# A GeGLU MLP on one core: four reorderings (pending gelu, w_down sums, first pair, last product)

## The chip, the cores and the metric

The kernel runs on one core of a Trainium2 chip. The metric is the device time of one execution in microseconds (us); three runs of the kernel before gave 2256.16, 2256.80 and 2257.91, median 2256.8.

## The reference

```python
x: (8, 1024, 1024)   w_gate, w_up: (1024, 4096)   w_down: (4096, 1024)   # float32
gate = x @ w_gate
up = x @ w_up
gate = 0.5 * gate * (1 + np.tanh(np.sqrt(2 / np.pi) * (gate + 0.044715 * gate ** 3)))
h = gate * up
return (h @ w_down).astype(np.float32)
```

## The kernel before, in words

**Passes.** The 8192 tokens are worked off in 8 passes of 1024 (`NPASS`, `TOK`). Each pass computes h for its tokens ("gate and up") and then the output ("down"). Operands are float16, sums are float32 in PSUM. The matrix products are done with fewer block products than the plain way, by sums and differences of blocks: passes 0 to 2 split every operand into 2x2 blocks and use 7 products in place of 8 (`gate_up_one`, `down`); passes 3 to 7 use operands split further, with 26 products for a group of four pairs' blocks (`gate_up_fast`, `quad`, `down_fast`). The operands of the later passes (sums of weight blocks) are made on the way in passes 0 to 2 and stored in DRAM: `wdop` from `wd_sums`/`wd_store` in pass 0, `wop` from `make_entry` in passes 1 and 2, `wdq` from `wd_unit`.

**Engines.** TensorE multiplies. ScalarE (ACT) copies PSUM banks, applies gelu and makes some entries; VectorE (DVE) adds PSUM to temporaries and forms operand sums; GpSimd (POOL) multiplies gelu by up and issues the weight loads (L336) and w_down loads (L394); SP issues the other transfers. Each engine executes its instructions in the order in which the program issues them: the order is written out by hand (`tc.manual_schedule()`, L241), and semaphores that the framework adds between engines do the waiting.

**A pair (L602 to L675).** In passes 0 to 2, one of the 16 pairs i of a pass covers two blocks of 128 gate and up columns. `SEQ` (L551) lists its 14 products: a name P1 to P7 and w (0 gate, 1 up). A product is 4 matmuls of 128x128 weights by 512 tokens (L626). It adds into the PSUM bank of its chain: P1, P6, P7, P4 share chain a, P5 and P3 chain b, P2 goes to chain c. After product k, `AFTER1` (L555) lists what the other engines do:

- after P1: "copy 0" and "copy 1" (L642, ScalarE): the bank of chain a is copied to a new bank c. P6, products 4 and 5, adds onto the a bank, so it must wait for these copies.
- P2 adds onto the banks that the copies wrote. In `SEQ` it stands late; the second pair of pass 0 uses `SEQ0` (L570), in which P2 makes products 3 and 4.
- "snap" (L637, ScalarE): a bank to a temporary; "add" (L645, VectorE): a bank plus a temporary; "gelu" (L650) and "gelu11", "gelu21" (L658), both ScalarE; "h11", "h21" (L663, VectorE); "prod" (L652, GpSimd).
- the last two, "add s2 0" and "add s2 1", come after products 13 and 14, the last of the pair. What follows them, "gelu s2" and "prod s2", is put into `pending` (L675) and issued by `flush()` in the next pair, after its product 2 and both copies (L671).

Between these stand `extra` steps: `sum_w` (L351, VectorE) forms the four weight sums of the next pair, in even pairs after products 3, 5, 7, 9, in odd pairs after 11 to 14; in passes 1 and 2 `make_entry` (L278 on VectorE, L374 on ScalarE) makes an entry after every second product, and `wd_unit` adds sums of its own (L278, L506).

**w_down in pass 0 (L708 to L719).** For n = 0 to 3, `wd_load` (four loads, GpSimd), `wd_sums` (four VectorE sums, L410 to L416) and `wd_store` (seven stores, SP) stand at slot s0 + ds, where slot 14 i + k is product k of pair i. With s0 = 28 n + 72 the sums stand in the even pairs 6, 8, 10 and 12.

**The first pair (L1191 to L1273)** of pass 0 starts from float32 inputs in DRAM. Loads of x and of the first weight columns are issued by SP at the start (L1275 to L1283); VectorE casts x (L297), TensorE transposes it (L303), VectorE and ScalarE copy the transposed blocks to SBUF (L305, L307), ScalarE casts weights (L331), and `products(mh, kh, c)` multiplies (L1198). The token half mh = 1 is transposed in two portions, each between two groups of products. `outputs` (L1210, L1211) makes the first blocks of h.

**The end (`down_fast`, L1063 to L1187).** `DOWN` (L118) lists products ("mul", 16 x 2 matmuls of 256 columns, L1099, both token halves m of one entry j after the other) and what is done with their banks: "snap" (L1156, ScalarE) and "acc" (L1168, VectorE), which adds a bank to a temporary; an "acc" with a last number of 0 or more is final, and its store (L1111, SP) is issued after the next product (`todo`). After the last product ("mul" 23) stand three final accs: two of the bank of product 22, then one of its own bank.

Of the kernel before, what the change touches and what calls it, by code (L numbers as in the profile page):

```python
# [11 lines left out]
ADD = mybir.AluOpType.add  # L12
SUB = mybir.AluOpType.subtract
# [8 lines left out]
OSC = 16.0  # L22
# [151 lines left out]
def kernel(  # L174
# [422 lines left out]
    def flush():  # L597
        for f in pending:
            f()
        pending.clear()  # L600

    def pair(p, i, extra, seq, after):  # L602
        bank = {}
        t = {}

        def ps(b, w):
            return ps_all[:, bank[b, w]]

        def tl(n):
            t[n] = tmp_free.popleft()  # L610
            return tmp[:, t[n]]

        def product(name, w):
            b = CHAIN[name]
            first = name in ("P1", "P5")
            if first:
                bank[b, w] = ps_free.popleft()
            o = W_OPERAND[name]
            if isinstance(o, tuple):
                e = (i % 2) * 2 * P + o[1] * P  # L620
                lhs = raw(p, i // 2)[:, w, o[0] * KH : (o[0] + 1) * KH, e : e + P]
            else:
                lhs = ssum(i)[:, o, w]
            rhs = xq[X_OPERAND[name]]
            for k in range(KH):
                nc.tensor.matmul(  # L626
                    ps(b, w), lhs[:, k], rhs[:, k, :],
                    start=(first and k == 0), stop=(k == KH - 1),
                    skip_group_check=True,
                )  # L630

        def do(what):
            op, *a = what.split()
            n = a[0] if a else None
            w = int(a[1]) if len(a) > 1 else 0
            if op == "snap":
                nc.scalar.copy(tl((n, w)), ps("a", w))  # L637
            elif op == "copy":

                w = int(n)  # L640
                bank["c", w] = ps_free.popleft()
                nc.scalar.copy(ps("c", w), ps("a", w))  # L642
            elif op == "add":
                o = tmp[:, t[n, w]]
                nc.vector.tensor_tensor(o, ps("b", w), o, ADD)  # L645
                if n == "s2":
                    ps_free.append(bank["b", w])
            elif op == "gelu":
                o = tmp[:, t[n, 0]]
                nc.scalar.activation(o, o, GELU, scale=GSC)  # L650
            elif op == "prod":
                nc.gpsimd.tensor_tensor(  # L652
                    hq[TO[n]][:, i, :], tmp[:, t[n, 1]], tmp[:, t[n, 0]], MUL
                )
                tmp_free.extend((t[n, 0], t[n, 1]))
            elif op in ("gelu11", "gelu21"):
                b = "c" if op == "gelu11" else "a"
                nc.scalar.activation(tl(b), ps(b, 0), GELU, scale=GSC)  # L658
                ps_free.append(bank[b, 0])
            elif op in ("h11", "h21"):  # L660
                b = "c" if op == "h11" else "a"
                h = hq["a11" if op == "h11" else "a12"]
                nc.vector.tensor_tensor(h[:, i, :], ps(b, 1), tmp[:, t[b]], MUL)  # L663
                tmp_free.append(t[b])
                ps_free.append(bank[b, 1])

        for k, (name, w) in enumerate(seq, 1):
            product(name, w)
            for what in after.get(k, ()):
                do(what)  # L670
            if k == 2:  # L671
                flush()
            for f in extra.get(k, ()):
                f()
        pending.extend([lambda: do("gelu s2"), lambda: do("prod s2")])  # L675
# [4 lines left out]
    def gate_up_one(p):  # L680
        unit_steps = {}
        if p in UNITS_ONE:
            free = deque(xc[:, j * 512 : (j + 1) * 512] for j in range(32, 38))
            free.append(spare)
            for u, s0, ds in UNITS_ONE[p]:
                load, fs = wd_unit(u, xc[:, 12288:16384], free)
                unit_steps[s0] = load
                for k, f in enumerate(fs):
                    unit_steps[s0 + 36 + ds * k] = f
        for i in range(NP):  # L690
            q, e = divmod(i, 2)
            extra = {k: [] for k in range(1, 15)}

            def at(k, f, *a):
                extra[k].append(lambda: f(*a))

            if p == 0 and i == 0:
                first_pair()
                continue
            if p == 0:  # L700
                if e == 1:
                    at(13, load_raw, p, q + 2)
                if 11 <= i < 15:
                    at(7, half_load, 0, 2 * (i - 11))
                if i >= 14:
                    at(4, half_load, 1, 4 * (i - 14))
                    at(6, half_load, 1, 4 * (i - 14) + 2)
                for n in range(4):  # L708

                    s0 = 28 * n + 72  # L710
                    for ds, f, a in (
                        (0, wd_load, (n, 0)), (2, wd_load, (n, 1)),
                        (4, wd_load, (n, 2)), (6, wd_load, (n, 3)),
                        (22, wd_sums, (0,)), (23, wd_sums, (1,)),
                        (24, wd_sums, (2,)), (25, wd_sums, (3,)), (26, wd_store, (n,)),
                    ):
                        pr, k = divmod(s0 + ds - 1, 14)
                        if pr == i:
                            at(k + 1, f, *a)  # L719
            elif i == 0:  # L720
                at(1, load_raw, p, 1)
            elif e == 1:

                at(13, load_raw, p, q + 2)

            ks = (3, 5, 7, 9) if e == 0 else (11, 12, 13, 14)
            for n, k in enumerate(ks):
                at(k, sum_w, p, i + 1, n)

            if FAST - 2 <= p < FAST:  # L730
                for j, n in enumerate(entries_of(p - FAST + 2)):
                    if j // 6 == e:
                        at(2 * (j % 6) + 2, make_entry, p, q, n)
            if (p, i) in ((0, 2), (FAST - 1, 13)):
                at(8, cast_x, p + 1)
            for k in range(14):
                if 14 * i + k in unit_steps:
                    at(k + 1, unit_steps[14 * i + k])
            if i == NP - 2:
                order[0] = [0, 1, 4, 2, 3, 5] if p % 2 == 0 else [2, 3, 4, 0, 1, 5]  # L740
                if p:
                    at(2, load_d, p, 0)
                    at(3, load_d, p, 1)
            if i == NP - 1:
                at(1, load_d, p, 2 if p else 0)
            second = p == 0 and i == 1
            pair(p, i, extra, SEQ0 if second else SEQ, AFTER0 if second else AFTER1)


# [313 lines left out]
    def down_fast(p):  # L1063
# [27 lines left out]
                ]  # L1091
            )

        def product(e, js):
            _, entry, h, c, first = e
            lhs, rhs = place[h], q_chunk(entry)
            for j in js:
                for m in range(2):
                    nc.tensor.matmul(  # L1099
                        ps_all[:, bank[c], m * MQ : (m + 1) * MQ],  # L1100
                        lhs[:, j, m * P : (m + 1) * P],
# [25 lines left out]
                product(e, js)  # L1127
        if p + 1 < NPASS:
            transpose_x(p + 1)
        count = 0  # L1130
        for i, e in enumerate(DOWN):
            if e[0] == "mul":
                count += 1
                if count > 2:
# [56 lines left out]
    def first_pair():  # L1191
        bank = {(mh, j, w): 4 * mh + 2 * j + w for mh in range(2) for j in range(2) for w in range(2)}

        def products(mh, kh, c):
            for w in range(2):
                for j in range(2):
                    for k in range(KH):
                        nc.tensor.matmul(  # L1198
                            ps_all[:, bank[mh, j, w], c],
                            raw(0, 0)[:, w, kh * KH + k, j * P : (j + 1) * P],  # L1200
                            xq[f"b{kh + 1}{mh + 1}"][:, k, c],
                            start=(kh == 0 and k == 0 and c.start == 0),
                            stop=(kh == 1 and k == KH - 1),
                            skip_group_check=True,
                        )

        def outputs(mh, j):
            t = tmp_free.popleft()
# [26 lines left out]
            f()  # L1235
        for w in range(2):
            cast_first(w, 1, slice(0, 256), nc.vector.tensor_copy)
        for kh in range(2):
            products(0, kh, slice(0, MH))
        for g in range(2):  # L1240
            x0_cast(1, g)
        for g in range(2):
            x0_transpose(1, g, 6 + g)
        for g in range(2, G):
            x0_cast(1, g)
        outputs(0, 0)
# [2 lines left out]

        nc.gpsimd.tensor_copy(mark, staging0(1, 0)[:, 0, 256:257])  # L1250
        load_raw(0, 1)
        for kh in range(2):
            products(1, kh, slice(0, MQ))
        for g in range(2, G):
            x0_transpose(1, g, g - 2)
        outputs(0, 1)
        for w in range(2):
            cast_first(w, 1, slice(256, 512))
# [64 lines left out]
```

## Time and profile before

| what | value |
| --- | --- |
| median of 3 runs | 2256.8 us |
| the profiled execution: time | 2256.16 us |
| the profiled execution: span | 2254.4 us |
| granted TensorE clock, mean | 1.000 |
| TensorE (PE) busy | 2246.1 us, 16634 matmuls |
| VectorE (DVE) busy | 1561.7 us |
| ScalarE (ACT) busy | 956.1 us |
| GpSimd (POOL) busy | 679.3 us |
| pass 1, gate and up / pass 2 | 193.39 us each |
| first matmul / end of the last | 1.59 us / 2250.1 us |

A line of a timeline gives the start in us, the time the group of instructions took in us, the engine, the line of the kernel, the operation, what it writes and reads, shapes and count; in brackets stands how long the engine had been idle and what ended that. A row of the waits gives who waited for whom, the total in us, how many times, and the longest. A row of the chain that ended last gives start and length in us, then engine, tile and line. A name such as L848 is a line of the code above; SPq and POOLq are transfers that these engines issue.

### The profile page before, as it was taken

The numbers are of one execution on the slowest core, as the hardware profiler recorded it, in microseconds if no ns is written. First come the engines' busy times: TensorE is split into PE (matmuls) and PEld (weight loads), VectorE is DVE, ScalarE is ACT, GpSimd is POOL, SyncE is SP. The second block draws the span as 40 slices with busy tenths as digits, with TensorE's granted clock in tenths as the row PEclk, the third lists the DMA queues.
The fourth block names the chain that finished last, engine by engine and source line by source line (L and its number), as shares of the span: only waits on it lengthen the run. The fifth ranks groups of instructions, "written<-read, shape, count | busy, mean of one in ns | idle before, by whom it ended". The sixth has DMA issues, their size and how long they took to land.

```text
span 2254.4 us, 42805 instructions
## 1 busy us (share of the span) xinstructions
PE 2246.1 (100%) x16634; PEld 1625.6 (72%) x16634; DVE 1561.7 (69%) x2190; ACT 956.1 (42%) x1866; POOL 679.3 (30%) x825
## 2 busy tenths in 40 slices
PE   9999999999999999999999999999999999999999
PEld 4444444444444445888888888888888888888888
DVE  6576458883588755777776677666786667866674
ACT  4444135651355622666125550356404653055520
POOL 1332013330133200555014550255403543044520
PEclk9999999999999999999999999999999999999999
DMA  9898969989999999999998999989999889988876
GB/s 241 163 207 218 284 184 241 263 264 283 255 227 249 282 309 349 328 342 370 302 339 274 317 304 318 322 270 324 311 324 316 285 308 326 311 311 277 289 285 225
DMA packets 308093, 642.46 MB, mean 285 GB/s; under 512 B 79088, under 2 KB 185328, under 8 KB 287344
## 3 DMA queue, kind: packets, MB, share of 16 engines
q1 hardware_dynamic: 253104, 566.57, 73.2%
q0 software_dynamic: 54784, 73.14, 19.3%
q8 instruction: 130, 2.13, 0.4%
q14 instruction: 75, 0.61, 0.1%
HBM read 574.36 MB, written 138.41 MB: 316 GB/s over the span
## 4 chain that ended last, share of the span: by engine, by line
PE 87%; DMA 2%; SPq 0%; DVE 0%; issue 0%; DVEq 0%
PE ps L848 40%; PE ps L1099 20%; PE ps L626 17%; PE ps L991 10%; DMA wd_quads<-x_sums 1%; SPq L255 0%; DMA ring<-wd_ops 0%; DVE x_sums L452 0%; DVE h_a L923 0%; DVE tmp L1168 0%; DVE x_sums L278 0%; SPq L487 0%; DVEq L278 0%; SPq L535 0%
## 5 line engine op out<-in xcount | busy, mean ns | idle before, releaser
L848 PEld LDWEIGHTS <-ring 128*128 128x128 f16 x8320 | 814.1, 98 | 94.4
L825 POOL TENSOR_TENSOR h_a<-tmp 128x256 f16<-128x256 f32 x640 | 469.3, 753 | 839.3 <-ACT tmp L813 831.9
L848 PE MATMUL ps<-x_sums,ring 128*128 128x256 f16 x5760 | 655.8, 273 | 0.0
L810 DVE TENSOR_TENSOR tmp<-tmp,ps 128x512 f32<-128x512 f32 x640 | 414.5, 683 | 148.1 <-PE ps L848 99.7
L626 PEld LDWEIGHTS <-ring 128*128 128x128 f16 x2632 | 257.5, 98 | 310.4
L795 ACT COPY tmp<-ps 128x512 f32<-128x512 f32 x520 | 304.1, 585 | 237.5 <-PE ps L848 162.8
L626 PE MATMUL ps<-x_sums,ring 128*128 128x512 f16 x1504 | 339.8, 379 | 0.0
L813 ACT ACTIVATE tmp<-tmp 128x256 f32<-128x256 f32 x640 | 264.1, 418 | 172.8 <-DVE tmp L808 79.4
L848 PE MATMUL ps<-x_b,ring 128*128 128x256 f16 x2560 | 305.6, 273 | 0.0
L808 DVE TENSOR_TENSOR tmp<-ps,tmp 128x512 f32<-128x512 f32 x240 | 165.4, 689 | 145.2 <-ACT tmp L795 101.0
L626 PE MATMUL ps<-x_b,ring 128*128 128x512 f16 x1128 | 259.1, 379 | 0.0
L652 POOL TENSOR_TENSOR h_a<-tmp 128x512 f16<-128x512 f32 x94 | 144.5, 1537 | 374.8 <-ACT tmp L650 271.9
L1099 PEld LDWEIGHTS <-h_a 128*128 128x128 f16 x2240 | 219.2, 98 | 25.4
L991 PE MATMUL ps<-ring,h_a 128*128 128x512 f16 x1024 | 222.3, 379 | 0.4 <-DMA ring<-wd_ops 0.4
L1099 PE MATMUL ps<-ring,h_a 128*128 128x256 f16 x1920 | 216.1, 273 | 0.0
L991 PEld LDWEIGHTS <-h_a 128*128 128x128 f16 x1152 | 112.7, 98 | 136.6 <-DMA ring<-wd_ops 0.9
L645 DVE TENSOR_TENSOR tmp<-ps,tmp 128x512 f32<-128x512 f32 x188 | 127.2, 683 | 112.6 <-ACT tmp L637 111.1
L1156 ACT ACTIVATE tmp<-ps 128x512 f32<-128x512 f32 x60 | 35.3, 597 | 362.6 <-PE ps L1099 274.6
L1168 DVE SCALAR_TENSOR_TENSOR tmp<-ps,tmp 128x512 f32<-128x512 f32 x120 | 81.1, 690 | 97.5 <-PE ps L1099 66.6
L351 DVE TENSOR_TENSOR ring<-ring 128x1024 f16<-128x1024 f16 x188 | 138.7, 751 | 11.1 <-DMA ring<-in_w_up_dram 6.9
L637 ACT COPY tmp<-ps 128x512 f32<-128x512 f32 x188 | 109.9, 586 | 77.8 <-PE ps L626 77.8
L1099 PE MATMUL ps<-ring,x_sums 128*128 128x256 f16 x1120 | 126.3, 273 | 0.0
(102 smaller groups left out, 1532.0 us busy)
## 6 DMA issues: line engine op xcount, KB each, us to landing
ring<-w_ops SPq DMA_DIRECT2D x480, 512.0 KB, 5.0
ring<-wd_quads SPq DMA_DIRECT2D x110, 1024.0 KB, 7.0
ring<-wd_ops SPq DMA_DIRECT2D x35, 1024.0 KB, 8.2
out_dram<-tmp SPq DMA_DIRECT2D x128, 256.0 KB, 6.6
w_ops<-h_s SPq DMA_DIRECT2D x128, 256.0 KB, 6.7
ring<-in_w_gate_dram POOLq DMA_DIRECT2D x23, 1024.0 KB, 10.5
ring<-in_w_up_dram POOLq DMA_DIRECT2D x23, 1024.0 KB, 17.8
wd_quads<-x_sums SPq DMA_DIRECT2D x131, 128.0 KB, 6.4
```

What stands on the lines that cost most here:

```text
L351: nc.vector.tensor_tensor(o, a, b, op)
L626: nc.tensor.matmul(ps(b, w), lhs[:, k], rhs[:, k, :], start=(first and k == 0), stop=(k == KH - 1), skip_group_check=True,)
L645: nc.vector.tensor_tensor(o, ps("b", w), o, ADD)
L652: nc.gpsimd.tensor_tensor(hq[TO[n]][:, i, :], tmp[:, t[n, 1]], tmp[:, t[n, 0]], MUL)
L795: nc.scalar.copy(tmp[:, t[o[1]]], ps_all[:, bank[o[2]]])
L808: nc.vector.tensor_tensor(d, b, a, SUB)
L810: nc.vector.tensor_tensor(d, a, b, ADD if o[4] == "add" else SUB)
L813: nc.scalar.activation(d, d, GELU, scale=GSC)
L825: nc.gpsimd.tensor_tensor(h, tmp[:, t[o[1]], MQ : 2 * MQ], g, MUL)
L848: nc.tensor.matmul(ps_all[:, bank[c], w * MQ : (w + 1) * MQ], lhs[:, w, k], rhs[:, k], start=(first and w == 0 and k == 0), stop=(k == KH ...
L991: nc.tensor.matmul(ps_all[:, bank[b, g]], lhs[:, j, g * P : (g + 1) * P], dc[:, n, :], start=(first and j == 0), stop=(j == NP - 1), skip_ ...
L1099: nc.tensor.matmul(ps_all[:, bank[c], m * MQ : (m + 1) * MQ], lhs[:, j, m * P : (m + 1) * P], rhs[:, j, :], start=(first and j == 0 and m ...
```

## The change

Four edits:

1. `flush()`, which issues the pending "gelu s2" (ScalarE) and "prod s2" (GpSimd) of the pair before, stands after product 1 and ahead of "copy 0", in place of after product 2 and behind "copy 1". This holds for all pairs of passes 0 to 2.
2. The w_down slots of pass 0 start 13 products earlier (28 n + 59), and the sums stand 4, the stores 3 slots closer to the loads: the loads go from the odd pairs 5, 7, 9 and 11 to the even pairs 4, 6, 8 and 10, and the sums from the even pairs 6, 8, 10 and 12 to products 7 to 10 of the odd pairs 5, 7, 9 and 11.
3. In the first pair, the two transpose portions of the second token half are put ahead of the last products of a group: the first ahead of the last 4 matmuls, the second ahead of the last 8.
4. In the last pass, the last product is done token half by token half (m = 0, then m = 1). Each half is followed by its own final acc on VectorE (128x256, new line 1147) and its own store of 128 KB (new line 1152). The two final accs of the bank of product 22, which stood ahead of the last acc, are now issued after both halves.

```diff
@@ pair
         for k, (name, w) in enumerate(seq, 1):
             product(name, w)
+            if k == 1:
+                flush()
             for what in after.get(k, ()):
                 do(what)
-            if k == 2:
-                flush()
@@ gate_up_one
-                    s0 = 28 * n + 72
+                    s0 = 28 * n + 59
                     for ds, f, a in (
                         (0, wd_load, (n, 0)), (2, wd_load, (n, 1)),
                         (4, wd_load, (n, 2)), (6, wd_load, (n, 3)),
-                        (22, wd_sums, (0,)), (23, wd_sums, (1,)),
-                        (24, wd_sums, (2,)), (25, wd_sums, (3,)), (26, wd_store, (n,)),
+                        (18, wd_sums, (0,)), (19, wd_sums, (1,)),
+                        (20, wd_sums, (2,)), (21, wd_sums, (3,)), (23, wd_store, (n,)),
@@ down_fast
-        def product(e, js):
+        def product(e, js, ms=range(2)):
...
-                for m in range(2):
+                for m in ms:
...
+        end = max(i for i, e in enumerate(DOWN) if e[0] == "mul") if p == NPASS - 1 else None
         count = 0
         for i, e in enumerate(DOWN):
+            if i == end:
+                finals = [f for f in DOWN[i:] if f[0] == "acc" and f[3] == e[3]]
...
+                for m in range(2):
+                    product(e, range(NP), (m,))
+                    if m == 0:
+                        for f in todo:
+                            f()
+                        todo.clear()
+                    c = slice(m * MQ, (m + 1) * MQ)
+                    for _, v, w, b, sc, st, o in finals:
...
+                        nc.vector.scalar_tensor_tensor(
+                            tmp[:, t[v], c], ps_all[:, bank[b], c], float(sc * OSC),
+                            tmp[:, t[w], c], MUL, ADD if st > 0 else SUB,
+                        )
+                        r0 = p * TOK + o // 4 * MQ + m * P
+                        nc.sync.dma_start(
+                            out=out2[r0 : r0 + P, o % 4 * MQ : (o % 4 + 1) * MQ],
+                            in_=tmp[:, t[v], c],
+                        )
+                continue
+            if end is not None and i > end and e in finals:
+                continue
@@ first_pair
-        def products(mh, kh, c):
-            for w in range(2):
-                for j in range(2):
-                    for k in range(KH):
+        def products(mh, kh, c, only=((0, 0), (0, 1), (1, 0), (1, 1))):
+            for w, j in only:
+                for k in range(KH):
...
-        for kh in range(2):
-            products(0, kh, slice(0, MH))
+        head, tail = ((0, 0), (0, 1), (1, 0)), ((1, 1),)
+        products(0, 0, slice(0, MH))
+        products(0, 1, slice(0, MH), head)
         for g in range(2):
             x0_cast(1, g)
         for g in range(2):
             x0_transpose(1, g, 6 + g)
+        products(0, 1, slice(0, MH), tail)
...
-        for kh in range(2):
-            products(1, kh, slice(0, MQ))
+        products(1, 0, slice(0, MQ))
+        products(1, 1, slice(0, MQ), ((0, 0), (0, 1)))
         for g in range(2, G):
             x0_transpose(1, g, g - 2)
+        products(1, 1, slice(0, MQ), ((1, 0), (1, 1)))
```

More of the change, by code (lines that the diff above doesn't have):

```diff
@@ L1129, in down_fast @@
             transpose_x(p + 1)
+        end = max(i for i, e in enumerate(DOWN) if e[0] == "mul") if p == NPASS - 1 else None
         count = 0
         for i, e in enumerate(DOWN):
+            if i == end:
+                finals = [f for f in DOWN[i:] if f[0] == "acc" and f[3] == e[3]]
+                for f in DOWN[i:]:
+                    assert f[0] != "snap" or f[2] != e[3]
+                for m in range(2):
[6 more added lines that the diff above has]
+                    for _, v, w, b, sc, st, o in finals:
+                        assert v == w and o >= 0
+                        nc.vector.scalar_tensor_tensor(
[10 more added lines that the diff above has]
+                continue
             if e[0] == "mul":
@@ L1192, in first_pair @@
         bank = {(mh, j, w): 4 * mh + 2 * j + w for mh in range(2) for j in range(2) for w in range(2)}
-        def products(mh, kh, c):
-            for w in range(2):
-                for j in range(2):
-                    for k in range(KH):
[L1198 to L1205, printed above, removed]
+        def products(mh, kh, c, only=((0, 0), (0, 1), (1, 0), (1, 1))):
+            for w, j in only:
+                for k in range(KH):
+                    nc.tensor.matmul(
+                        ps_all[:, bank[mh, j, w], c],
+                        raw(0, 0)[:, w, kh * KH + k, j * P : (j + 1) * P],
+                        xq[f"b{kh + 1}{mh + 1}"][:, k, c],
+                        start=(kh == 0 and k == 0 and c.start == 0),
+                        stop=(kh == 1 and k == KH - 1),
+                        skip_group_check=True,
+                    )
         def outputs(mh, j):
```

## Prediction

> **What bounds the kernel now.** I read the engine totals first, then TensorE's waits, then the chain that ended last.
>
> ```profile
> span 2254.4 us, 42805 instructions
> PE 2246.1 (100%) x16634; PEld 1625.6 (72%) x16634; DVE 1561.7 (69%) x2190; ACT 956.1 (42%) x1866; POOL 679.3 (30%) x825
> ```
> ```profile
> PE ps L1219 <- DVE h_s L1222: 1.6, 1, 1.6
> PE ps L1198 <- DVE x_b L305: 1.1, 2, 0.6
> PE ps L1198 <- ACT ring L331: 0.6, 1, 0.6
> PE ps L991 <- DMA ring<-wd_ops: 0.4, 1, 0.4
> PE ps L303 <- DVE h_a L297: 0.2, 1, 0.2
> ```
> ```profile
> 307.50 193.39 PE ps L626 x896
> 500.88 96.69 PE ps L991 x448
> 597.57 193.39 PE ps L626 x896
> ...
> 2159.26 90.84 PE ps L1099 x832
> 2250.10 0.02 issue
> 2250.12 0.69 DVE tmp L1168
> ```
>
> TensorE has five waits in 2.25 ms, 3.9 us together. From 307 us on the chain is matmuls touching each other: 193.39/896 = 0.216 us for one of 512 columns, 90.84/832 = 0.109 us for one of 256. So the change can win little (the two 0.6 us waits at L1198, and some of the 4.3 us after the last matmul), and any new TensorE wait lands in the time undiminished.
>
> **Part 1, the early flush.** A pair is 14 products of 4 matmuls: 14 x 0.863 = 12.09 us. Call the start of its first matmul T. The pending gelu of the pair before (ACT, L650) moves ahead of "copy 0" and "copy 1" (ACT, L642). ScalarE works in order, so copy 0 now queues behind a gelu that waits for VectorE's "add s2 0" (L645) of the pair before. Behind copy 0 stands TensorE: the fourth product, P6, adds onto the bank that copy 0 reads, and nothing behind it can start. P6 begins at T + 12 x 0.216 = T + 2.59.
>
> ScalarE and VectorE around the pair with T = 391.94:
>
> ```profile
> 393.00 0.57 ACT L642 COPY ps<-ps 128x512 f32<-128x512 f32 x1 [2.91 <-PE ps L626]
> 393.92 0.57 ACT L642 COPY ps<-ps 128x512 f32<-128x512 f32 x1 [0.35 <-PE ps L626]
> 394.40 0.63 ACT L650 ACTIVATE tmp<-tmp 128x512 f32<-128x512 f32 x1
> ...
> 413.62 0.63 ACT L650 ACTIVATE tmp<-tmp 128x512 f32<-128x512 f32 x1 [0.96 <-DVE tmp L645]
> 414.15 0.58 ACT L658 ACTIVATE tmp<-ps 128x512 f32<-128x512 f32 x1
> ```
> ```profile
> 393.36 1.28 DVE L645 TENSOR_TENSOR tmp<-ps,tmp 128x512 f32<-128x512 f32 x2
> 394.56 0.41 DVE L278 TENSOR_TENSOR spare<-x_sums 128x512 f16<-128x512 f16 x1
> 394.89 0.68 DVE L278 TENSOR_TENSOR h_s<-h_s,ring 128x1024 f16<-128x1024 f16 x1
> 395.49 1.76 DVE L278 TENSOR_TENSOR x_sums<-h_s 128x1024 f16<-128x1024 f16 x1
> 398.80 0.69 DVE L645 TENSOR_TENSOR tmp<-ps,tmp 128x512 f32<-128x512 f32 x1 [1.55 <-ACT tmp L637]
> ```
>
> Now copy 0 runs at T + 1.06, as soon as its product is there, though VectorE finishes the first add only at 393.36 + 0.68 = T + 2.10. In the new order the gelu starts 0.04 after the add (the row at 413.62: the add before it ended at 413.58), the next ScalarE instruction 0.53 later (414.15), the copy takes 0.57, and TensorE follows a releaser by 0.05 (a VectorE copy ending at 20.12 started the matmul at 20.17). With L the end of the add after T, P6 can start at L + 1.19, so **it stalls by L - 1.40 wherever L is above 1.40**; here by 0.70.
>
> I read L at each pair from the timelines. Pass 1, into pairs 1 to 15: 1.34 1.37 0.36 1.41 1.68 1.42 2.10 2.16 2.27 1.74 1.85 1.41 2.09 1.41 1.68. Pass 2: 1.34 1.37 1.64 1.74 1.61 1.41 2.09 1.41 1.28 1.74 1.61 1.41 1.68 1.41 1.68. Pass 0: at most 1.42. These passes are late because there VectorE also makes the `w_ops` entries (L278) between the adds.
>
> Excesses are not simply added. From pair 3 on VectorE idles (waits for ScalarE or TensorE) in odd pairs alone, at T + 6.86 and T + 9.77; from there it runs without a gap to the second next odd pair. So a stall in an even pair lets it catch up for the odd pair after it, and each group of an even and an odd pair costs the larger excess of the two. Pass 1, groups (4,5) to (14,15): 0.28 + 0.70 + 0.20 + 0.45 + 0.69 + 0.28 = 2.6; group (8,9) would be 0.87, but its lateness starts at an idle that ends with a DMA (403.09 us), which a 0.7 us stall one pair earlier absorbs, so 0.2. Pass 2, (2,3) to (14,15): 0.24 + 0.34 + 0.69 + 0.01 + 0.34 + 0.28 + 0.28 = 2.2. **Sum +4.8.** Earlier gelus and products on GpSimd help nobody on the path.
>
> The bounds: what decides L in the odd pairs is the 1.76 us row above. It is a VectorE sum of 0.68 us, drawn out because GpSimd's product (L652) ran at that moment. In even pairs such a row falls into the gapless stretch, 1.07 us each time. GpSimd starts there after its two weight-load issues (L336, ending about T + 3.23), which don't move, so I keep the stretch. Were it gone everywhere, only the even pairs' own excesses stay, about 1.2; were each group's two excesses to add, 6.6.
>
> [...]
>
> **Part 2, the w_down sums 13 products earlier.** Same instructions: 16 loads on GpSimd (0.57 us to issue), 16 VectorE sums (0.68; L412 0.92), 28 stores on SP. The order moves the sums from even to odd pairs of pass 0. The first of four now stands before the add at L645 that waits for ScalarE (T + 6.86) and runs in that idle time; the others put the later adds of the odd pair back by 0.84 + 2 x 0.60 less the 1.70 that VectorE has free there now (0.34), so L in pairs 6, 8, 10, 12 goes from 0.77 to about 1.12, still under 1.40. The loads landed by 89.03 (first store) after issue from 81.47; issued a pair earlier they are due at about 77, before use. SP has nothing else then. **0**; if the first sum doesn't find the idle time, L is 1.72: 0.3 x 4 = +1.3.
>
> **Part 3, the first pair.** The two waits at L1198 are TensorE waiting for copies of freshly transposed x. With matmuls put behind the transposes (0.86 us each time), it is busy meanwhile: the first gap shrinks by 0.52, the second by some 0.7, so the last products could start at 24.04 instead of 25.23. But ScalarE isn't moved:
>
> ```profile
> 24.52 1.04 ACT L331 CAST ring<-x_sums 128x1024 f16<-128x1024 f32 x1 [0.46 <-DMA x_sums<-in_w_up_dram]
> 25.47 1.07 ACT L307 COPY x_b<-ps 128x512 f16<-128x512 f16 x2
> 26.43 0.61 ACT L1210 ACTIVATE tmp<-ps 128x512 f32<-128x512 f32 x1
> 26.92 2.00 ACT L331 CAST ring<-h_a 128x1024 f16<-128x1024 f32 x2
> 28.80 1.10 ACT L1210 ACTIVATE tmp<-ps 128x512 f32<-128x512 f32 x2
> 29.85 0.57 ACT L642 COPY ps<-ps 128x512 f32<-128x512 f32 x1
> ```
>
> It runs without idle time from the landing of a weight block (24.52) to copy 0, which ends at 30.42. The products' second half needs the L307 copies, ending 26.54 (new wait), and the second pair's third product, P2, adds onto what copy 0 writes, so it starts at 30.47; it starts there now (28.72 + 8 x 0.216 = 30.45). The gain of 1.1 us is given back whole: **0**, between -0.4 (copy 0 not last) and +0.1.
>
> **Part 4, the split last product.** Three things. (a) In the built program the first matmul of the second token half waits for VectorE's read of the first half: both lie in one bank. TensorE waits from the last matmul of half one: 0.27 (its length) + 0.02 + d + 0.05 - 0.11, with d the 128x256 VectorE read. No such row exists; below is half of 0.69 (0.35), above 0.69 itself (L1168). I take 0.42, the 128x512 f16 PSUM copies of L305, the nearest in bytes: +0.66. (b) In before, VectorE does the two other final sums (0.60 + 0.69) during the last product (at 2246.63) and one after it (2250.12). Now the half reads stand ahead of them, so after the last matmul come half a read (0.34), 0.60 and 0.69: 0.94 more than 0.69. (c) The last store, 256 KB instead of following 2.9 us behind another one, follows by 0.6 us; two such at 2247.3 ended 0.17 later than a lone one. **+1.8**, from +1.1 (no bank wait) to +2.3 (d = 0.69).
>
> [...] No row of before has a read inside a product. [...]
>
> **Sum**: 4.8 + 0 + 0 + 1.8 = +6.6 on the profiled execution's 2256.2 (its span 2254.4 and 1.8 around it), 2262.8. That execution is the lowest of three, 0.6 under the median, so **2263.4** as a median. A measurement of this kernel can tell about 0.2%, 4.5 us, from no change.
>
> **Rivals.** *Stretch lost*: in passes 1 and 2 GpSimd's shifted products no longer draw out VectorE's sums, L falls by 1.07 in odd pairs, below 1.40; part 1 costs 1.2, total 2256.8 + 3.0 = 2259.8: not slower by the bound. [...] *Hidden*: the flush costs nothing, because the gelu isn't held up; then only the tail counts, 2258.6; against it stands ScalarE's order. *The gains hold*: the flush is free, ScalarE's chain shortens with TensorE's, so part 3 gives 1.1, and the half reads shorten the tail by 0.3: 2255.4; against it the DMA at 24.52. *Stalls add*: the groups' excesses add (6.6) and pass 0 stalls too (1.3): 2266.5.
>
> **Numbers.** Forecast (2261.4 to 2265.5) 0.66; stretch lost 0.16; hidden 0.07; gains hold 0.02; stalls add 0.08; a gain that I don't see 0.01. Range 2258.5 to 2265.9: it takes in "stretch lost" and the ends of parts 1 and 4. The likeliest case's own range is 2261.4 to 2265.5. Slower by over 0.2% (above 2261.3): 0.74; within (stretch lost, hidden, gains hold): 0.25; faster: 0.01, for TensorE waits only 3.9 us in all.
>
> **What would show it.** New TensorE waits at L626 on ScalarE's L642, some 14 of 0.1 to 0.7 us, in passes 1 and 2 alone; chains of those passes above 193.39 by 2.6 and 2.2; the pair after the first pair still starting its third product near 30.5; one TensorE wait on VectorE before the last 16 matmuls; three VectorE rows after the last matmul. No waits at L626 would make the prediction wrong; so would a third product at 30.1.

## The result and the profile after

The kernel after takes 2263.34 us (median of 6 runs, 2262.54 to 2265.24), beside 2256.48 us for the kernel before (median of 6, 2255.86 to 2259.28; the three runs named ahead of the prediction are among them). The ratio is 1.0029, with a 95% interval from 1.0016 to 1.0042: slower by 6.9 us. The profiled execution of after took 2263.72 us, its span is 2262.0 us, 7.6 us more than that of before.

The engine totals of after, from its page:

```profile
span 2262.0 us, 42808 instructions
PE 2248.7 (99%) x16634; PEld 1625.5 (72%) x16634; DVE 1569.0 (69%) x2191; ACT 954.9 (42%) x1866; POOL 683.8 (30%) x825
```

The matmuls are the same 16634, and PE's busy time grew by 2.6 us only, so most of the 7.6 us is time in which TensorE stood still. TensorE's waits in after (total, times, longest):

```profile
PE ps L626 <- DVE tmp L645: 2.2, 7, 0.4
PE ps L626 <- ACT ps L642: 1.9, 4, 0.5
...
PE ps L991 <- DMA ring<-wd_ops: 1.0, 1, 1.0
...
PE ps L1099 <- DVE tmp L1147: 0.5, 1, 0.5
```

Three things differ from before. There are eleven new waits at the pairs' products (L626) and one inside the last product (L1099), and the two waits on VectorE's x copies (L305, 1.1 us) are gone. A wait here is counted from the modelled end of the last matmul; counted from the moment at which the product would have started in an unbroken row, each costs some 0.17 us more (0.40 shown, 0.56 late), so the sums below are made with starts of matmuls.

The chain that ended last, in after, is whole again only behind the pairs of passes 1 and 2:

```profile
471.32 33.85 PE ps L626 x156
505.17 96.69 PE ps L991 x448
...
2255.13 1.92 PE ps L1099 x16
```

In before one row of 193.39 us stood for pass 1 and another for pass 2. Here the pairs of a pass fall into pieces (the 33.85 us are 156 matmuls), with VectorE's rows between them, and a piece of 16 matmuls stands by itself at the end.

Where the 7.6 us are, by the starts of the matmuls in the two traces:

| stage | after less before, us | the prediction's term |
| --- | --- | --- |
| first pair, to the third product of the second pair (30.47 to 29.42) | -1.06 | 0 |
| pass 0, pairs 6, 8, 10 and 12, four stalls of 0.56 | +2.25 | 0 |
| between pass 0's pairs and pass 1's (97.29 to 97.82) | +0.53 | none |
| pass 1, pairs | +2.57 | +2.6 |
| pass 2, pairs | +1.99 | +2.2 |
| last product, wait for the half read | +0.68 | +0.66 |
| from the last matmul to the end (4.31 to 4.92) | +0.61 | +1.11 |
| sum | +7.57 | +6.6 |

Nothing shows the 0.53 us to be part of the change: it belongs to one wait for a w_down operand load (L991, 0.4 us in before and 1.0 in after), and the same stretch took 96.83 to 97.96 us in the kernels below that leave that step as it was.

### The profile page after: what moved, and what is told of

It is laid out like the page before. It is cut to its first block, busy times and chain, and to the rows that moved or that the text cites. A ratio compares the mean times of both kernels' runs of the same rounds, so it can differ in the third digit from the quotient of the medians.

```text
span 2262.0 us, 42808 instructions
## 1 busy us (share of the span) xinstructions
PE 2248.7 (99%) x16634; PEld 1625.5 (72%) x16634; DVE 1569.0 (69%) x2191; ACT 954.9 (42%) x1866; POOL 683.8 (30%) x825
## 4 chain that ended last, share of the span: by engine, by line
PE 83%; DVE 3%; DMA 2%; issue 1%; SPq 0%; ACT 0%; DVEq 0%; ACTq 0%
PE ps L848 40%; PE ps L1099 20%; PE ps L626 13%; PE ps L991 10%; DMA wd_quads<-x_sums 1%; DVE ring L351 1%; DVE h_s L278 1%; DVE tmp L645 1%; DMA w_ops<-h_s 1%; SPq L255 0%; DMA ring<-wd_ops 0%; DVE h_a L663 0%; DVE x_sums L278 0%; ACT ps L642 0%; DVE tmp L1147 0%
## 5 line engine op out<-in xcount | busy, mean ns | idle before, releaser
L626 PEld LDWEIGHTS <-ring 128*128 128x128 f16 x2632 | 257.3, 98 | 317.5 <-issue 8.7
L626 PE MATMUL ps<-x_sums,ring 128*128 128x512 f16 x1504 | 342.3, 379 | 4.3 <-DVE tmp L645 2.2
L652 POOL TENSOR_TENSOR h_a<-tmp 128x512 f16<-128x512 f32 x94 | 149.1, 1586 | 378.0 <-ACT tmp L650 263.2
L626 PE MATMUL ps<-x_b,ring 128*128 128x512 f16 x1128 | 259.3, 379 | 0.0
L1099 PEld LDWEIGHTS <-h_a 128*128 128x128 f16 x2240 | 219.1, 98 | 26.1 <-issue 0.7
L991 PE MATMUL ps<-ring,h_a 128*128 128x512 f16 x1024 | 222.3, 379 | 1.0 <-DMA ring<-wd_ops 1.0
L1099 PE MATMUL ps<-ring,h_a 128*128 128x256 f16 x1920 | 216.3, 273 | 0.5 <-DVE tmp L1147 0.5
L991 PEld LDWEIGHTS <-h_a 128*128 128x128 f16 x1152 | 112.7, 98 | 137.1 <-DMA ring<-wd_ops 1.4
L351 DVE TENSOR_TENSOR ring<-ring 128x1024 f16<-128x1024 f16 x188 | 133.3, 722 | 9.4 <-DMA ring<-in_w_up_dram 4.8
L1099 PE MATMUL ps<-ring,x_sums 128*128 128x256 f16 x1120 | 126.4, 273 | 0.0
```

The costliest lines, as they stand in the source:

```text
L351: nc.vector.tensor_tensor(o, a, b, op)
L626: nc.tensor.matmul(ps(b, w), lhs[:, k], rhs[:, k, :], start=(first and k == 0), stop=(k == KH - 1), skip_group_check=True,)
L652: nc.gpsimd.tensor_tensor(hq[TO[n]][:, i, :], tmp[:, t[n, 1]], tmp[:, t[n, 0]], MUL)
L991: nc.tensor.matmul(ps_all[:, bank[b, g]], lhs[:, j, g * P : (g + 1) * P], dc[:, n, :], start=(first and j == 0), stop=(j == NP - 1), skip_ ...
L1099: nc.tensor.matmul(ps_all[:, bank[c], m * MQ : (m + 1) * MQ], lhs[:, j, m * P : (m + 1) * P], rhs[:, j, :], start=(first and j == 0 and m ...
```

## The experiments

**The four edits one by one.** Each of these is the kernel before with one edit of the diff. All four ran in one session, beside 31 runs of the kernel before with a median of 2256.58 us.

```diff
 # e1_flush: edit 1
             product(name, w)
+            if k == 1:
+                flush()
...
 # e2_slots: edit 2
-                    s0 = 28 * n + 72
+                    s0 = 28 * n + 59
...
 # e3_first: edit 3
...
+        products(0, 1, slice(0, MH), tail)
...
 # e4_tail: edit 4
+                for m in range(2):
+                    product(e, range(NP), (m,))
...
```

> The early flush alone. My theory: it costs about 4.6 us (2.6 in pass 1, 2.0 in pass 2, as TensorE waits ahead of P6), nothing in pass 0, because there the first add ends at most 1.42 us after a pair's start when the w_down sums stay in the even pairs: 2261.1 against 2256.5. The rival, that pass 0's waits in the changed kernel come from the flush itself, gives 4.6 + 2.2 = 6.8: 2263.3.

Measured: 2260.77 us (2259.53 to 2262.03), ratio 1.0017 [1.0008, 1.0027]. Pass 0 lost nothing, pass 1 2.59 us, pass 2 1.74 us. The flush accounts for 4.2 us of the medians, and the rival in which the flush by itself makes the waits of pass 0 (6.8) falls.

> The earlier w_down slots alone, the flush behind the copies as before. My theory: the sums in the odd pairs make the first add end about 1.9 us after the start of pairs 6, 8, 10 and 12 as in the changed kernel, but nothing on TensorE's path waits for that add when the copies go first: 0.0, 2256.5, and no wait ahead of P6. The rival, that the slots cost by themselves (transfers or VectorE), gives +2.2: 2258.7.

Measured: 2256.83 us, ratio 1.0000 [0.999, 1.0009], and no stall in any pair. The moved w_down sums cost nothing by themselves.

> The reordered transposes of the first pair alone. By the prediction 0, because ScalarE's chain from a weight block's landing (24.52 us) to copy 0 decides; the second pair would start its third product near 30.5. The rival, which the changed kernel's profile suggests (second pair started at 27.56 in place of 28.72), gives -1.1: 2255.4; then the landing must be earlier too, by the edit or by chance: the first pair of the three other kernels of this call is as before and shows how far the landing scatters.

Measured: 2256.03 us (2254.58 to 2256.43), ratio 0.9996 [0.9986, 1.0006]. The time can't tell; the profile has the third product of the second pair at 30.12 us, where before has 30.47 and e1_flush 31.10. That is taken up below.

> The split last product alone. My theory: +1.3 to +1.8 (TensorE waits 0.6 us for the half read, then three reads after the last matmul in place of one), 2257.8 to 2258.3. The rival, that shorter stores at the end pay for it, gives 0 or below: 2256.5 or less.

Measured: 2258.11 us (2257.17 to 2259.13), ratio 1.0007 [0.9998, 1.0017]; from the last matmul to the end 4.91 us, where before and the first three have 4.29 to 4.31.

The differences of the four medians add to 4.2 + 0.25 - 0.55 + 1.5 = 5.4 us, and the whole change costs 6.9. The difference of 1.5 us could be noise, since each of the four intervals is about 4 us wide. The traces decide it: the four stalls of pass 0 stand in none of these four kernels, so they show only where edits meet.

**Flush and w_down slots together.** In the next two kernels, and wherever it is said below, x of passes 1 to 7 is loaded untransposed: loads of the same size, other numbers.

```diff
 # e5c: edits 1 and 2, nothing else
 # e7c: the same, with the fourth w_down sum one product later
-                        (20, wd_sums, (2,)), (21, wd_sums, (3,)), (23, wd_store, (n,)),
+                        (20, wd_sums, (2,)), (22, wd_sums, (3,)), (23, wd_store, (n,)),
```

> The early flush and the earlier w_down slots together, first pair and last product as before. In this kernel and the two beside it the x of passes 1 to 7 is loaded by plain transfers of the same bytes and not transposed (the output is another one for that reason); the pairs of passes 0 to 2 keep every instruction, so the waits inside them are compared, not the time. My theory: flush and slots cost more together than alone, because the slots make the adds of pairs 6, 8, 10 and 12 late and the early flush makes TensorE wait for them: four waits of 0.56 us in pass 0, 2.2 to 2.4 together, and 4.3 to 4.6 in passes 1 and 2. The rival, that pass 0's waits in the changed kernel come from its shifted first pair: none in pass 0.

Measured (one run): four stalls of 0.56 us in pass 0, 2.24 us together; pass 1 2.57, pass 2 1.74. Edit 1 alone lost 0 there and edit 2 alone 0: it is the two together. The timeline of after shows what happens ahead of the stalled pair 6:

```profile
85.26 1.27 POOL L652 TENSOR_TENSOR h_a<-tmp 128x512 f16<-128x512 f32 x1 [6.93 <-ACT tmp L650]
85.30 1.77 DVE L416 TENSOR_TENSOR h_s<-h_s 128x1024 f16<-128x1024 f16 x1
...
89.39 0.68 DVE L645 TENSOR_TENSOR tmp<-ps,tmp 128x512 f32<-128x512 f32 x1
...
90.11 0.63 ACT L650 ACTIVATE tmp<-tmp 128x512 f32<-128x512 f32 x1 [4.44 <-DVE tmp L645]
...
91.27 2.10 PE L626 MATMUL ps<-x_sums,ring 128*128 128x512 f16 x9 [0.40 <-DVE tmp L645]
```

Look at the fourth w_down sum (L416): it takes 1.77 us, where the three before it took 0.68 or 0.69. GpSimd's product began 0.04 us ahead of it. VectorE has no idle time from there to "add s2 0" (89.39), which so ends 1.95 us after the pair's start; the flushed gelu follows it (90.11), copy 0 the gelu, and P6 starts at 91.27. The row of P6 names VectorE's second add as its releaser, which ended within 0.1 us of copy 0. It is not what P6 waits for: in e2_slots the second add ends as late (3.15 us after the start of pair 6), and P6 starts at 2.59 without a wait. By the prediction's own rule the stall is 1.95 - 1.40 = 0.55. In e2_slots the four L416 sums take 1.77 us as well, but there the copies stand ahead of the gelu and don't wait for the add: that is why edit 2 alone shows nothing.

> Flush and slots, but the fourth w_down sum one product later (behind h21 in place of ahead of it), so that it no longer starts in the moment in which GpSimd multiplies; x loaded by plain transfers, not transposed. My theory: that sum took 1.77 us in place of 0.68 because of GpSimd, and this 1.1 us makes the four waits of pass 0; moved, the add ends near 1.4 to 1.5 us after the pair's start and the waits shrink from 0.56 to 0.1 us or less. The rival, that the number of sums in the odd pairs makes the adds late: waits near 0.5 as before.

Measured (one run): pass 0 lost 0.27 us, 0.14 of it in each of pairs 1 and 2 and none in the four pairs. Its waits at the pairs' products:

```profile
PE ps L627 <- ACT ps L643: 1.6, 3, 0.5
...
PE ps L627 <- DVE tmp L646: 0.6, 3, 0.2
```

(In this kernel the code lines stand one further down.) One product later the fourth sum starts at 88.03, when GpSimd's product (86.88, 1.27 us) is nearly over; ahead of it VectorE has h21 (L664, 0.69 us at 87.43, from PSUM) and 0.42 us of idle time. The sum takes 0.68 us, and the four stalls are gone with nothing else moved. So the sum took 1.77 us where it started 0.04 us behind the product, and 0.68 us where it started 1.15 us behind it. The 1.09 us between them are less than the product's 1.27; what holds the sum up inside them, no row shows.

**What makes the stalls of passes 1 and 2.** The theory says that the early flush stalls because VectorE makes a `w_ops` entry between a pair's last adds. So the entry after product 12 was moved behind them. Both kernels below have edit 1 as well.

```diff
-                        at(2 * (j % 6) + 2, make_entry, p, q, n)
 # e6c: in all pairs of passes 1 and 2 (x untransposed)
+                        at((2, 4, 6, 8, 10, 14)[j % 6], make_entry, p, q, n)
 # e6d: not in the odd pairs of pass 1 (x untransposed)
+                        at(14 if j % 6 == 5 and (p == 2 or e == 0) else 2 * (j % 6) + 2, make_entry, p, q, n)
```

> The early flush without the slots, and in passes 1 and 2 the entry that VectorE makes after product 12 moved behind product 14, so behind the two adds of s2; x loaded by plain transfers, not transposed. My theory: the flush costs only because the add ends late; the move takes one 0.60 us sum out from ahead of it, the latest pairs fall from 2.07 to 1.47, the others under 1.40: TensorE's waits in passes 1 and 2 shrink from 4.3 to some 0.3 us. The rival, that the gelu ahead of the copies costs whatever VectorE does: 4.3 as in the flush alone.

Measured (one run): 2312.91 us. Pass 2 went as expected, from 1.74 to 0.22 us lost. Pass 1 lost 56.5 us, in waits up to 7.4 us, through a fault of the experiment. In the odd pairs of pass 1 that entry reads a raw weight block, and the load issued after product 13 (L336) overwrites this block. Behind product 14 the entry had to wait for the load, with all of VectorE's later work behind it (VectorE stood ahead of six sums at L279 for 50.8 us together, up to 10.3; before has no such row). The waits make up 42.6 of the 56.5 us; the other 14 go with PE's busy time, 2260.4 us in place of 2246.1 for the same 16634 matmuls, and with a granted clock of 8 tenths in two of the 40 slices of its page (404 to 520 us), where that of before has 9 in all.

> The early flush alone, with the w_ops entry that stands after product 12 moved to after product 14, so that in those pairs no entry sum stands between the last adds: in pass 2 in all pairs, in pass 1 in the even pairs alone (in the odd pairs of pass 1 that entry reads a raw weight block which the load issued after product 13 overwrites; there it stays at 12). x of passes 1 to 7 is loaded untransposed (the work and its times are of the same size, the numbers computed are not the reference's). Theory (the stall is L - 1.40, and L is late because VectorE makes an entry between the adds): pass 2 loses 0.2 to 0.3 in place of 1.74 to 2.0; in pass 1 the stalls into odd pairs (0.49, 0.69, 0.11, 0.69 with the flush alone) fall to 0 to 0.1 each, the one into pair 10 (0.36), behind an odd pair, stays: 0.4 to 0.6 in place of 2.6; no wait over 1 us at the pairs' products. Rival (the gelu's place alone stalls TensorE, whatever VectorE does): passes 1 and 2 lose 2.6 and 1.7 as before.

Measured (one run): 2257.59 us; pass 2 lost 0.22. In pass 1 the stalls into pairs 3, 7, 11 and 13 (0.49, 0.69, 0.11, 0.69) fell to 0, 0.08, 0 and 0.08, and the one into pair 10 stayed at 0.36, all as expected; but pass 1 lost 1.72, not 0.4 to 0.6, since pair 8 now stalls for 0.96 and a further 0.18 at P6's second half. VectorE and TensorE of e6d ahead of it and in it (two views):

```profile
402.89 0.69 DVE L352 TENSOR_TENSOR ring<-ring 128x1024 f16<-128x1024 f16 x1 [0.88 <-DMA ring<-in_w_up_dram]
```
```profile
407.18 4.65 PE L627 MATMUL ps<-x_sums,ring 128*128 128x512 f16 x20 [0.80 <-DVE tmp L646]
```

VectorE waited for a weight load before the weight sums of pair 8, as it does in before at 403.09. The prediction counted this group at 0.2 because a stall of 0.7 one pair earlier gives the load time to land, and at 0.87 without that. With the earlier stall down to 0.08, the wait is back and 0.96 comes, which fits that account. One execution doesn't prove it, since the landing scatters: in the eight profiles that keep the old order of passes 1 and 2, VectorE's wait at this place was 0.69 us in before, 0.36, 0.14 and 0.11 in three others, and nothing in four. By the prediction's rule the size is right (L 2.35 less 1.40 is 0.95).

**The first pair.** In the nine profiles of kernels without edit 3 and without the added load below, the third product starts 19.95 to 20.10 us after ScalarE's first weight cast; in the three with it (after, e3_first, e10_best) 18.71 to 18.87. So the edit wins 1.1 to 1.2 us, once the varying landing of the first weights is taken out. Copy 0 in e1_flush (ScalarE's timeline):

```profile
30.48 0.57 ACT L642 COPY ps<-ps 128x512 f32<-128x512 f32 x1 [0.65 <-PE ps L626]
```

ScalarE, with all casts done, waits 0.65 us for TensorE here, so time that TensorE wins counts. In the profile that the prediction read, the same row (29.85) shows no wait. The two differ by a landing: the third weight cast starts 11.1 us after the first in e1_flush, five other kernels without edit 3 and all three with it, and 12.5 to 12.7 us after it in before, e7c and e8b_tail_order. To see the edit with a late landing, 512 KB of x were loaded ahead of these weights, into a place that nothing reads (x of passes 1 to 7 untransposed):

```diff
     for c in (slice(0, 256), slice(256, 512)):
+        if c.start:
+            nc.sync.dma_start(out=hf["s3"][:, 6144:8192].bitcast(FP32), in_=x2[0:P, :])
```

> The kernel before, with one added load of 512 KB (128 rows of x into a part of h's buffers that nothing reads) on SP ahead of the second halves of the first weight columns: at some 350 GB/s these weights land about 1.4 us later. Counted from the first weight cast: third cast at 12.5 to 14, third product of the second pair at 20.1 to 21.5, set by ScalarE's chain from the landing to copy 0, which runs without a wait for TensorE.

Measured (one run): 2256.11 us; third cast 12.61 and third product 20.02 us after the first cast, 7.41 between them. Copy 0 waits for nothing. As expected.

> Edit 3 (the first pair) alone, with the same added load of 512 KB ahead of the second halves of the first weight columns. Theory (edit 3 gains where TensorE is late, and nothing where the weights' landing sets ScalarE's chain): counted from the third weight cast, the third product comes as long after it as in the kernel before with the same load, within 0.2 us; counted from the first cast it stands 0 to 0.3 us earlier, if the landings agree. Rival (TensorE's 1.1 us are won in any case): 0.9 to 1.2 us earlier by both counts.

Measured (one run): 2258.07 us; third cast 13.94, third product 22.67 us after the first cast, 8.73 between them. Neither theory: counted from the third cast, the third product comes 1.3 us later with the edit than without it. ScalarE's and TensorE's rows, then two rows of its table by windows (the last columns: granted TensorE clock, DMA share, GB/s):

```profile
27.91 3.42 PE L1198 MATMUL ps<-x_b,ring 128*128 128x256 f16 x16 [2.07 <-ACT x_b L308]
...
32.45 0.57 ACT L643 COPY ps<-ps 128x512 f32<-128x512 f32 x1 [1.23 <-PE ps L627]
```
```profile
28.00:29.00 1.00, 1.00 (x7) 0.70 (x7) 0.61 (x2) 1.00 (x2) 0.48 (x1) 0.55 0.68 88
...
30.00:31.00 1.00, 1.00 (x7) 0.68 (x5) 0.91 (x3) 1.00 (x3) 0.00 (x0) 0.50 1.21 196
```

TensorE ran out of products early and stood for 2.07 us, until ScalarE, behind the late casts, had copied the transposed x. After that its clock was granted at 0.55 (28 to 29 us) and 0.50 (29 to 31 us), and a matmul of 256 columns took some 0.21 us (3.42 for the 16) in place of 0.109; from 31 to 32 us the table has 0.74, from 32 on 1.00. Copy 0 then waited 1.23 us for it. Less that wait, the third product comes 7.50 us after the third cast, beside 7.41 without the edit: that agrees with ScalarE's chain setting the time with a late landing, as the prediction had it, and the clock comes on top. The landings of the two runs (12.61, 13.94) didn't agree, so how the edit does at 12.6 is still open, and so is whether the kernel without the edit would keep its clock at 13.94.

**The tail in another order.** The two final sums of product 22's bank are issued ahead of the half reads.

```diff
 # e8b_tail_order: edit 4 alone, with
+                product(e, range(NP), (0,))
...
+                for _, v, w, b, sc, st, o in [f for f in DOWN[i:] if f[0] == "acc" and f not in finals]:
...
+                for m in range(2):
+                    if m == 1:
+                        product(e, range(NP), (m,))
...
 # e10_best: edit 3, and the last product in one piece, then the two sums of
 # product 22's bank, then its own sum in two halves with their 128 KB stores
+                product(e, range(NP))
...
```

> Only the split last product, with the two final sums of the product before it kept ahead of the half reads. My theory: TensorE's wait for the first half read stays (0.5 us), but after the last matmul stands only a half read (0.42) in place of 0.69, and its store is half as long; the tail from the last matmul falls from 4.3 (4.9 in the split as changed) to about 3.7: together -0.1, 2256.5, 1.5 under the split alone. The rival, that the wait of TensorE is the whole cost of the split, leaves it at 2257.1 or more and the tail at 4.3.

Measured: 2255.99 us (median of 10) beside 2256.74, ratio 0.9999 [0.9989, 1.0008]. From the last matmul to the end 3.22 us in place of 4.91 (some 3.7 was expected), with the wait inside the product still 0.52. After the last matmul one VectorE row is left:

```profile
2252.11 0.42 DVE L1155 SCALAR_TENSOR_TENSOR tmp<-ps,tmp 128x256 f32<-128x256 f32 x1 [2.00 <-PE ps L1099]
```

Compare the same place in after, where the two sums of 0.60 and 0.69 stand behind it:

```profile
2254.65 0.42 DVE L1147 SCALAR_TENSOR_TENSOR tmp<-ps,tmp 128x256 f32<-128x256 f32 x1 [3.89 <-PE ps L1099]
...
2255.13 1.91 PE L1099 MATMUL ps<-ring,h_a 128*128 128x256 f16 x16 [0.52 <-DVE tmp L1147]
...
2257.07 0.42 DVE L1147 SCALAR_TENSOR_TENSOR tmp<-ps,tmp 128x256 f32<-128x256 f32 x1 [2.00 <-PE ps L1099]
2257.41 1.28 DVE L1195 SCALAR_TENSOR_TENSOR tmp<-ps,tmp 128x512 f32<-128x512 f32 x2
```

So the tail of after loses by the order of VectorE's work more than by the split, which costs 0.68 us by its wait.

> The kernel before with the reordered first pair, and with the last product in its old order of matmuls, the two other final sums ahead, its own final sum read in two halves with a 128 KB store each. My theory: the first pair gives 0.5 (0 to 1.1 by when the weights land); at the end one half read more (0.34) against a store half as long: the tail from the last matmul, 4.3 before and 3.2 with the split product in the good order, becomes about 3.6, without TensorE's wait of 0.5: -0.7. Together -1.2: 2255.4, ahead of both kernels. The rival, that tail and first pair scatter more than they give, leaves it at 2256.6.

Measured: 2255.76 us (median of 11, 2254.24 to 2257.38) beside 2257.09 (14), ratio 0.9994 [0.9985, 1.0003]. Its span of 2252.5 us is the shortest of all profiled executions, the tail 3.70 us, and TensorE waits nowhere at L626 or L1099. The interval includes 1: the two gains, 1.1 and 0.6 us by the traces, are too small for a measurement of this kernel.

## Why the prediction was right or wrong

The forecast, 2263.4, lies beside the measured 2263.3, and its mechanism was the main one: the gelu moved ahead of the copies makes TensorE wait. But the nearness of the numbers is partly luck. From one profiled execution to the other the prediction had +6.6 and the traces have +7.6, and inside that two terms, parts 2 and 3, were wrong in opposite directions; the tail cost 0.5 us less than forecast, and 0.53 us came from a load that no term names. (The prediction's five waits of TensorE are five rows with six waits; nothing rests on that.)

- **Part 1, right.** 2.57 and 1.99 us against 2.6 and 2.2; alone 2.59 and 1.74. (The 1.74 is lower by a group of 0.25 at pair 3.) The largest groups came as worked out: into pair 7 0.68 for 0.70, (10,11) 0.46 for 0.45, pair 13 0.68 for 0.69 in pass 1; 0.25, 0.36, 0.69, 0.36 and 0.27 for 0.24, 0.34, 0.69, 0.34 and 0.28 in pass 2. Three groups' stalls of 0.28 didn't come, since L fell (1.68 to 0.82, and twice to 0.59), and one of 0.48 came into pair 3 of pass 1, where L rose from 0.36 to 1.87. There a sum of VectorE took 1.99 us (at 336.31) beside a product of 1.28 us on GpSimd (336.45), where in before the product took 4.08 us (334.74) beside VectorE's sum of 0.69 (334.59). In both VectorE's sum started first, by 0.14 and 0.15 us, so which of the two starts first doesn't settle which takes longer. The longer sum doesn't need the flush: in the eight profiles with the old order L into this pair is 0.36 in three and 1.64 or 1.65 in five. So which of the small groups stalls changes from execution to execution (pair 5 in place of 3 in e5c, neither in e7c), and the list of L, read from one execution, fixes only the large ones. In after there were 11 stalls in passes 1 and 2, not 14. The profile puts part of them down to VectorE's second add, which ends with copy 0, in place of the copy. The "stretch lost" rival was true of the three groups alone. e6d shows, in one run, that the entry between the adds is what makes the odd pairs' stalls.
- **Part 2, the mis-sized term.** 0 predicted, +2.25 measured. The step of the prediction that failed is "L in pairs 6, 8, 10, 12 goes from 0.77 to about 1.12": it counted each moved sum at its undisturbed 0.60 to 0.84, though part 1 had just said that a VectorE sum that meets GpSimd's product takes 1.76. The fourth took 1.77, and L came to 1.95. The upper end that was named (1.72, +1.3) was too low as well. The sign "in passes 1 and 2 alone" fell with it. The loads were not there by 77: the first sum was released by one at 79.77, but still ran in the idle time.
- **Part 3, wrong for most executions.** 0 predicted, -1.06 measured; the sign of being wrong that it named ("so would a third product at 30.1") came true with 29.42. The failed step is "the gain of 1.1 us is given back whole". The chain that it read was there, in an execution whose weights had landed 1.5 us later than in most; it took one profile for the rule. The bound of -0.4 was too tight for the same reason.
- **Part 4, right in its two main terms.** The wait cost 0.68 for 0.66 and the read took 0.42, as taken from the nearest row by bytes; VectorE's part after the last matmul grew by 0.93 for 0.94. The store, expected 0.17 later, was done 0.32 sooner after VectorE's last row (3.26 us against 3.58). That is the same in e4_tail; why, no run here tells.

## What to carry to other kernels

Work that is moved forward in an engine's program order brings its own wait with it (the flushed gelu, 4.2 us in e1_flush): ask what it waits for and who stands behind it, and measure the slack there before the move. Two edits that are each free at one place (here in pass 0, 0 and 0 us alone, 2.24 together in e5c) can together use up more than its slack, so a duration that depends on what another engine does at that moment (the w_down sum, 0.68 or 1.77 us) is to be taken at its long value when the work is moved. And a step whose answer hangs on a DMA's landing (here 11.1 or 12.5 to 12.7 us after the first cast) is read from several executions, not from one.

## What the runs showed of the hardware that was not expected

- After 2.07 us without a matmul (e12_first_late, up to 27.91) the granted clock was 0.55 from 28 to 29 us, 0.50 from 29 to 31, 0.74 from 31 to 32 and 1.00 from 32 on.
- In e8b_tail_order 1.88 us without a matmul, up to 9.09, was followed by a granted clock of 1.00 in each stretch of its table up to 14 us. In e6c TensorE waited six times for VectorE's add, 41.6 us together and up to 7.4 at once, and its page has the granted clock at 8 tenths in two slices (404 to 520 us). No run varies the idle time, so what sets these cases apart is not shown.
- The second half of the first weights landed in two ways, 11.1 us (22.25 less 11.15 in e1_flush) or 12.5 to 12.7 us (23.02 less 10.37 in before) after the first by the casts, in kernels that load them alike.
